# The low parts of float32 weights: subtracted anew for the second sequence, or written to DRAM by the first and loaded by the second

## The chip, the core and the metric

The kernel runs on one core of one Trainium2 chip. The metric is the device time of one execution in microseconds (us). The kernel before has a median of 3235.25 us over 3 runs (3233.89 to 3237.98).

## The reference

Two sequences of 512 tokens and 1024 channels go through a trunk of two layers, with one set of weights for both. A layer is

```python
h = rms_norm(x, ln1_g);  z = h @ w_in            # 1024 -> 2816, split over four mixers
y = [s5(z), hyena(z), rwkv7(z), na(z)]           # 256 channels each
x = x + concat(rms_norm(y_g, grp_g)) @ w_out     # 1024 -> 1024
h = rms_norm(x, ln2_g)
x = x + square(relu(h @ w_mlp1)) @ w_mlp2        # 1024 -> 4096 -> 1024
```

Everything is float32. The mixers are a complex diagonal scan in two directions (S5), a long convolution by spectra (Hyena), a recursion with a state per head in two directions (RWKV-7), and attention in a window of 8 by 16 tokens.

## The kernel before

**Dense products.** Each float32 operand is taken as the sum of two parts: `hi`, the value rounded to 12 significant bits, and `lo`, the rest. `mm3` adds three products for each pair of 128x128 weights and 128x512 activations: w_hi h_hi (L1392), w_hi h_lo (L1393) and w_lo h_hi (L1394). A weight tile is [128, 4, 128], 256 KB, and takes part in 12 matrix multiplications of 512 columns.

**Weights.** `load_w` (L1372 to L1384) loads one tile, raw, and makes both parts: ScalarE (ACT) rounds it to `hi` (`split`, L297), and GpSimd (POOL) or VectorE (DVE) subtracts (L298), so that `lo` lies where the raw tile was. Every fourth tile is subtracted on DVE, the others on POOL. Seven buffers hold tiles: three for `hi`, four for the raw tile that becomes `lo`. A load waits until PE is done with the tile four places before it. For one sequence a layer takes 188 tiles: 44 of w_in, 16 of w_out, 64 of w_mlp1 and 64 of w_mlp2. Each sequence loads and splits all of them in both layers: 376 tiles a sequence, 752 in all.

**Order of the work.** The dense products run as one stream: w_in of the first layer for sequence 0, then for sequence 1; then w_out, the MLP and the next layer's w_in of sequence 0; the same of sequence 1; w_out and MLP of the second layer of sequence 0; of sequence 1. The mixers of one sequence run beside the dense products of the other. A scheduler sets each engine's order when the program is built; on the chip each engine goes through its own queue in order. SyncE (SP) issues every DMA, in order: a DMA whose wait is not over holds up those behind it. In the MLP a tile of results leaves PSUM by DVE (L1535, and L1536 squares it), is split by ACT (L297) and DVE (L298), and w_mlp2's products are added to x by DVE (L1545).

Of the kernel before, what the change touches and what calls it, by code (L numbers as in the profile page):

```python
# [5 lines left out]
F32 = mybir.dt.float32  # L6
# [6 lines left out]
P = 128  # L13
T = 1024          # tokens: both sequences, side by side
# [9 lines left out]
ROUND = 12582912.0          # 1.5 * 2**23: adding and taking it off rounds to an integer  # L24
# [3 lines left out]
# vectors by channel of one layer, packed as columns of a [128, NPAR] tile  # L28
# [19 lines left out]
def tiled(w, nk, n):  # L48
    """[DEPTH, K, N] -> [DEPTH, N / n, K / (128 nk), 128, nk, n]: what one transfer takes lies together."""
    L, k, m = w.shape  # L50
    return w.reshape(L, k // (P * nk), nk, P, m // n, n).transpose(0, 4, 1, 3, 2, 5)


# [1 line left out]

def pack_params(inp):
    """[DEPTH, 128, NPAR_IN]: column j of a vector holds its channels 128 j .. 128 j + 127."""
    out = np.zeros((DEPTH, P, NPAR_IN), np.float32)
    for n, c in _PAR:
        a = np.asarray(inp[n])  # L60
        for l in range(DEPTH):
            v = a[l].reshape(-1)
            if n in ('na_q_g', 'na_k_g'):
                v = np.concatenate([v, v])
            out[l, :, POFF[n]:POFF[n] + c] = v.reshape(c, P).T
    return out


def s5_layout(inp):
    """[DEPTH, 128 (group parity, state), ...]"""  # L70
# [3 lines left out]
    def sc(x):          # (L, 2, 16, 64) -> (L, 128, 16 = (pair, dir))  # L74
        return x.reshape(DEPTH, 2, 8, 2, 64).transpose(0, 3, 4, 2, 1).reshape(DEPTH, P, 16)

    def mb(x):          # (L, 2, 16, 64, 16) -> (L, 128, 16, 16)
        return x.reshape(DEPTH, 2, 8, 2, 64, 16).transpose(0, 3, 4, 2, 1, 5).reshape(DEPTH, P, 16, 16)
# [7 lines left out]
def na_bias(inp):  # L86
    """[DEPTH, head pair, 128 queries (row, col 16), case 3, head 2, 256 keys (row 8, col 32)]: the table's entries
    by position, the constant -1e30 outside the window."""
# [16 lines left out]
def constants():  # L105
# [13 lines left out]
    # DFT at the half-odd multiples of 1/1024 below 1/8, tokens 4 s + j  # L119
    th = 2 * np.pi * (np.arange(128) + 0.5) / 1024  # L120
    ang = np.arange(512)[:, None] * th[None]
    cs = np.stack([np.cos(ang), -np.sin(ang)], 1).reshape(128, 4, 2, 128)       # s, j, (re, im), f
    c['hy_fw'] = np.concatenate([cs, -cs[:, 3:]], 1)
    c['hy_iv'] = (cs * (2.0 / 1024)).transpose(3, 1, 2, 0)                      # f, j, (re, im), s
# [11 lines left out]
def place(nc):  # L136
    """Where the memory that Mem hands out begins: it ends with SBUF."""
# [5 lines left out]
class Mem:  # L143
    """Parts (lo, hi) of the big tile, in units of 1 KB per partition, the first ones preferred: views are
    handed out and given back in program order, and Tile orders the accesses to them."""
# [48 lines left out]
class Ctx:  # L194
    """Pools, constants and small helpers shared by the parts of the kernel."""
# [46 lines left out]
    def rsqrt(self, x, n, tag):  # L242
        """x [128, n] (SBUF) -> 1/sqrt(x): a first guess by the exponent, within 3.5%; a step of third order (the
        best coefficients for that range), which leaves 3e-5; and one of Newton."""
# [15 lines left out]
    def token_rstd(self, srcs, ntok, sel, add, tag, sc=1.0, mulc=None):  # L260
        """srcs: squares, tiles [128 ch, ntok]; sums over the channels that sel [128, w] picks (and over
        the tiles if w is 1) -> 1/sqrt(sums * sc + add), [128 tok, ntok / 128, tiles * w]."""
# [16 lines left out]
    def head_bcast(self, rn, M, tag):  # L279
        """rn [128 tok, 4, heads 2] view of one channel tile -> PSUM [128 ch, 512 tok]."""  # L280
# [9 lines left out]
    def bcast(self, rn, pb):  # L290
        """rn [128 tok, n] -> PSUM pb [128, n * 128], the same on every partition."""
# [3 lines left out]
    def split(self, hi, lo, x, eng):  # L295
        """hi + lo = x: hi has 12 significant bits, lo the rest."""
# [10 lines left out]
# A step works on 8 chunks at once: 4 of the forward direction (slots 0-3) and 4 of the backward one  # L307
# (slots 4-7, in token order); two steps a sequence. The two recursions over chunks run side by side.

def rw_shift(K, par, zp, i, out):  # L310
    """zp [128, 514], zero at the ends -> out = (1 - mu) z + mu / 2 (prev + next)."""
# [7 lines left out]
def rw_load(K, zr, i, n, M):  # L319
    """n tiles of channels of one sequence."""  # L320
# [5 lines left out]
def rw_seq(K, l, par, zr, M):  # L326
    """One sequence. zr: DRAM [1024 ch, 512 tok] (r, k, v, wd + ad, gd, shifted) -> [128, 2, 512]."""
    nc = K.nc
    k = rw_load(K, zr, 2, 2, M)
    # kk / 2, normalised over each head  # L330
# [31 lines left out]
def rw_wa(K, l, zr, M):  # L362
    """What the decays and a are made of, in two parts: [128, 2, (w2 over a2 | tanh wd over ad), 512]."""
# [3 lines left out]
    w2 = ww[:, 0].rearrange("p (d c) -> p d c", d=2)        # rows 0-63: w2, rows 64-127: a2  # L367
# [10 lines left out]
def rw_step(K, l, par, g, zr, prep, y, st, M, beside):  # L378
    """Forward chunks 4 g .. 4 g + 3, backward ones 7 - 4 g .. 4 - 4 g; y [128, 2, 512] is set (g = 0)
    or added to (g = 1); st: the states [128, 2 dir, 2 tiles, 64]. Returns the new ones. beside: a generator,  # L380
    run beside the chunks."""
    nc = K.nc

    def tok(x):             # [128, 512] by token -> [128, dir, 256]
        x = x.rearrange("p (d t) -> p d t", d=2)
        return x[:, ::-1] if g else x

    def tok4(x):            # -> [128, dir, 4 chunks, 64]
# [3 lines left out]
    def s3(x):              # by slot  # L392
# [9 lines left out]
    for c in range(2):  # L402
# [16 lines left out]
        # log decays / -exp(-1/2), summed up within the chunk  # L419
# [6 lines left out]
        ep = ep_[:, :, 0:66]        # columns 0 and 65 are 1  # L426
# [8 lines left out]
        b_t = M([P, 8, 2, 64])      # (b, k) on the even head's partitions, (k, b) on the odd one's  # L435
# [23 lines left out]
    # scores of every slot and head, by token of b or k (partitions) and of a or r  # L459
# [15 lines left out]
    # inverse of I - N, the backward ones transposed: first its blocks of 16, one on each partition (block in the pair,  # L475
    # slot, tile, parity, pair); a 64 x 64 matrix takes 4160 words, so that the blocks of the diagonal lie 1040 apart
    d1 = K.d([32 * 4160], "rw_d1", 2)               # slot, tile, parity
# [38 lines left out]
    # blocks of 32: with R1, R2 on the diagonal and Q of N off it, R1 Q R2 is off it; half of R1's rows a partition  # L516
# [22 lines left out]
    rc = M([P, 2, 16, 32])          # (parity, pair, row); the inverse, its transpose; (slot, tile), column  # L539
# [13 lines left out]
    # blocks of 64: rows lo that N's block has, columns hi that it fills  # L553
# [39 lines left out]
    # values by token: even heads at partitions 64.., odd heads at 0..; U fills the other half  # L593
# [19 lines left out]
    # what the values add to W  # L613
# [13 lines left out]
    # the chunks, one after the other  # L627
    for i in range(4):
        next(beside, None)
        sl = slice(i, 8 - i, 7 - 2 * i)         # slots i and 7 - i  # L630
# [58 lines left out]
def rw_bonus(K, l, par, zr, out, M):  # L689
    """The bonus and the gate, [128, 2, 512] each."""  # L690
# [52 lines left out]

def s5_ops(K, l, M, tag):
    """Operators of one layer, to DRAM: B [128 (t, c), pair, re/im, dir, 128], C [128 (re/im, n), pair,
    parity, dir, 128 (t, c)], lag matrices [16 groups, 16 c, 15 lags x 16]. Returns them and a^8."""
# [23 lines left out]
    # (a - 1) / lambda  # L770
# [15 lines left out]
    def pairs(re, im):  # L786
        """[re | re] and [im | -im]: products with (x, y), the second's halves swapped, add up."""
# [12 lines left out]
    GD = K.d([4, 2, 2, 16, 240], f"s5_gd{l}")        # pair % 4, pair // 4, parity, c, lags  # L800
    for half in range(2):
        yield from s5_half(K, l, half, f2, a2, sB, sC, GD, M, tag)
    # a^8 for the recursion over chunks, laid out (ri, pair, dir)
# [17 lines left out]
def s5_half(K, l, half, f2, a2, sB, sC, GD, M, tag):  # L821
    """The operators of 4 of the 8 pairs of groups."""
# [8 lines left out]
    def cmul(out, x, ri, conj):  # L831
        """out = x * (r + i im), views [128, 8 (ri, pair), 2 (dir), 16]."""
# [16 lines left out]
    for j in range(8):  # L849
        bj = BAv[:, :, 7 - j:9 + j:2 * j + 1]        # forwards at 7 - j, backwards at 8 + j  # L850
# [21 lines left out]
    for j in range(9):  # L872
        cj = CAv[:, :, j:18 - j:17 - 2 * j]          # forwards at j, backwards at 17 - j
# [14 lines left out]
    # lag matrices  # L888
# [25 lines left out]
def s5_front(K, l, zd, M):  # L914
    """One sequence. zd: DRAM [16 groups, 16 c, 8 t, 64 chunks] -> the inputs by chunk and the states."""
# [3 lines left out]
    SS = M([P, 2, 8, 130])          # the forward states at 1 .. 64, the backward ones at 65 .. 128  # L919
# [33 lines left out]
    # from (parity, n), re/im to (re/im, n), parity  # L953
# [10 lines left out]
def s5_back(K, l, par, zd, front, M, tag):  # L964
    """Returns [128, 2, 512]."""
# [3 lines left out]
    ys = M([P, 8, 4, 2, 16])        # (pair // 4, chunk), t, pair % 4, parity, c  # L969
    for q in range(2):  # L970
        L = M([P, 8, P])            # pair % 4, pair // 4
# [3 lines left out]
        py = K.p([P, 4, P], tag)   # (pair // 4, chunk), pair % 4, (t, c)  # L975
        for j in range(4):
            Cop = M([P, 2, 2, P])   # pair // 4, dir
# [28 lines left out]
    # gelu(x) = x (1 + tanh(sqrt(2/pi) (x + 0.044715 x^3))) / 2  # L1006
# [9 lines left out]
    for c in range(2):  # L1016
# [6 lines left out]
        # columns are (t, chunk), the output's (chunk, t)  # L1023
# [8 lines left out]
def reduce_angle(K, x, k):  # L1032
    """x -> x - 2 pi round(x / 2 pi), within [-pi, pi]; k: scratch like x."""
# [795 lines left out]
```

## Time and profile before

The profiled execution has a span of 3230.3 us from its first to its last instruction; the profile gives no other time of its own for it. The three timed runs lie 3.6 to 7.7 us above that span.

| engine | busy us | share of the span |
|---|---|---|
| PE (TensorE) | 2989.3 | 93% |
| DVE | 2222.3 | 69% |
| POOL | 1222.8 | 38% |
| ACT | 1054.7 | 33% |

From the order of SP's loads the dense stream stands so in the trace (start of the first load of each piece, us): w_in of layer 1 for sequence 0 at 6 and for sequence 1 at 226; w_out 472, MLP 658 and w_in of layer 2 at 1217, all for sequence 0; the same for sequence 1 at 1403, 1478 and 2043; then w_out 2239 and MLP 2310 of sequence 0, and w_out 2819 and MLP 2861 of sequence 1, which is the end. So the second sequence's tiles are loaded from 226 to 472, from 1403 to 2239 and from 2819 on.

A busy share is a mean over stretches with different limits, so the stretches are looked at apart. PE's busy time counts waiting inside a matrix multiplication's own latency too; in the last stretch, where PE has nothing but dense products, one of 512 columns starts every 0.227 us. DMA counts are of the core's 16 DMA engines together.

### The profile page before, as it was taken

The numbers are of one execution on the slowest core, as the hardware profiler recorded it, in microseconds if no ns is written. First come the engines' busy times: TensorE is split into PE (matmuls) and PEld (weight loads), VectorE is DVE, ScalarE is ACT, GpSimd is POOL, SyncE is SP. The second block draws the span as 40 slices with busy tenths as digits, with TensorE's granted clock in tenths as the row PEclk, the third lists the DMA queues.
The fourth block names the chain that finished last, engine by engine and source line by source line (L and its number), as shares of the span: only waits on it lengthen the run. The fifth ranks groups of instructions, "written<-read, shape, count | busy, mean of one in ns | idle before, by whom it ended". The sixth has DMA issues, their size and how long they took to land.

```text
span 3230.3 us, 48385 instructions
## 1 busy us (share of the span) xinstructions
PE 2989.3 (93%) x17328; PEld 2329.1 (72%) x17328; DVE 2222.3 (69%) x4431; ACT 1054.7 (33%) x1934; POOL 1222.8 (38%) x963
## 2 busy tenths in 40 slices
PE   7998898789899998998889999788999999999999
PEld 5676776667677776676667777677777777888887
DVE  8987993774884879648957366868775486544443
ACT  5333233342222334333222233333332233332222
POOL 6644430332323346453333233443333243343333
PEclk9999888799999999998999999899989999999999
DMA  5464253252334334543324333346234333433333
GB/s 162 145 160 151 98 144 93 74 115 77 89 100 143 92 117 140 153 144 93 90 72 106 102 115 108 105 137 167 76 74 117 111 115 101 126 110 98 95 98 108
DMA packets 361397, 365.23 MB, mean 113 GB/s; under 512 B 175014, under 2 KB 215590, under 8 KB 360136
## 3 DMA queue, kind: packets, MB, share of 16 engines
q1 hardware_dynamic: 361160, 362.14, 38.6%
q8 instruction: 140, 2.29, 0.3%
q14 instruction: 97, 0.79, 0.1%
HBM read 305.06 MB, written 54.10 MB: 111 GB/s over the span
## 4 chain that ended last, share of the span: by engine, by line
PE 39%; DVE 14%; DMA 2%; issue 2%; ACT 1%; SPq 1%; POOL 0%; DVEq 0%; ACTq 0%; POOLq 0%
PE pd L1392 10%; PE pd L1394 10%; PE pd L1393 10%; DVE m L1167 1%; DVE m L298 1%; PE ra L675 1%; DVE m L530 1%; PE ra L673 1%; PE ra L467 1%; DVE m L950 1%; DVE m L512 1%; DVE s_t L946 1%; DVE s_t L949 1%; DVE m L1545 1%; DVE do L1535 0%
## 5 line engine op out<-in xcount | busy, mean ns | idle before, releaser
L298 POOL TENSOR_TENSOR m<-m,m 128x512 fp32r<-128x512 f32 x564 | 793.4, 1409 | 1480.2 <-ACT m L297 1432.4
L1392 PE MATMUL pd<-m,m 128*128 128x512 f32 x2984 | 1225.8, 411 | 108.1 <-ACT m L297 36.0
L1394 PE MATMUL pd<-m,m 128*128 128x512 f32 x2984 | 1212.6, 407 | 14.9 <-POOL m L298 9.8
L1393 PE MATMUL pd<-m,m 128*128 128x512 f32 x2984 | 1211.9, 406 | 2.7 <-DVE m L298 2.1
L297 ACT CAST m<-m 128x512 fp32r<-128x512 f32 (+1 forms) x776 | 488.2, 632 | 1112.8 <-PE pd L1393 401.7
L1392 PEld LDWEIGHTS pd<-m,m 128*128 128x128 f32 x2984 | 581.8, 195 | 264.7 <-issue 68.9
L1394 PEld LDWEIGHTS pd<-m,m 128*128 128x128 f32 x2984 | 581.3, 195 | 160.9 <-POOL m L298 16.3
L1393 PEld LDWEIGHTS pd<-m,m 128*128 128x128 f32 x2984 | 581.4, 195 | 132.8 <-issue 9.1
L1545 DVE TENSOR_TENSOR m<-pd,m 128x512 f32<-128x512 f32 x256 | 175.1, 686 | 234.7 <-PE pd L1394 234.1
L298 DVE TENSOR_TENSOR m<-m,m 128x512 fp32r<-128x512 f32 (+1 forms) x212 | 172.6, 814 | 116.6 <-ACT m L297 116.1
L1535 DVE SCALAR_TENSOR_TENSOR do<-pd,R 128x512 f32<-128x512 f32 x128 | 87.7, 687 | 112.5 <-PE pd L1394 104.3
L297 ACT CAST m<-do 128x512 fp32r<-128x512 f32 x128 | 79.4, 620 | 237.2 <-DVE do L1536 237.1
L1167 DVE TENSOR_TENSOR m<-m,m 128x512 f32<-128x512 f32 (+1 forms) x224 | 154.2, 724 | 1.1 <-POOL m L1167 0.8
L298 DVE TENSOR_TENSOR m<-do,m 128x512 fp32r<-128x512 f32 x128 | 101.5, 794 | 45.1 <-ACT m L297 44.5
L1536 DVE TENSOR_TENSOR do<-do 128x512 f32<-128x512 f32 x128 | 129.5, 1013 | 2.6
L467 PE MATMUL ra<-m,m 64*128 64x128 f32 x512 | 73.4, 335 | 22.1 <-DVE m L451 12.4
L467 PEld LDWEIGHTS ra<-m,m 64*128 64x128 f32 x512 | 62.7, 229 | 37.8 <-issue 20.4
L946 DVE TENSOR_TENSOR s_t<-m,s_AI 128x32 f32<-128x32 f32 x252 | 81.6, 324 | 7.3 <-ACT m L935 1.8
L950 DVE TENSOR_TENSOR m<-m,s_t 128x32 f32<-128x32 f32 x252 | 83.1, 330 | 5.0
L675 PE MATMUL ra<-m,m 128*64 128x64 f32 x512 | 79.0, 248 | 0.0
L840 POOL TENSOR_TENSOR m<-m,s5p_i 128x256 f32<-128x256 f32 x64 | 57.8, 903 | 55.0 <-DVE m L842 31.1
L1423 DVE SCALAR_TENSOR_TENSOR m<-m,par,m 128x512 fp32r<-128x512 f32 x64 | 67.4, 1062 | 15.9 <-ACT m L1422 15.8
(351 smaller groups left out, 3609.5 us busy)
## 6 DMA issues: line engine op xcount, KB each, us to landing
m<-in_w_mlp SPq DMA_DIRECT2D x512, 256.0 KB, 2.6
m<-in_w_in SPq DMA_DIRECT2D x176, 256.0 KB, 2.8
m<-zr SPq DMA_DIRECT2D x36, 512.0 KB, 4.0
m<-in_w_out SPq DMA_DIRECT2D x64, 256.0 KB, 2.9
m<-in_xT SPq DMA_DIRECT2D x32, 256.0 KB, 4.3
zr<-do SPq DMA_DIRECT2D x32, 256.0 KB, 2.1
m<-hy_spec SPq DMA_DIRECT2D x8, 1024.0 KB, 5.1
m<-s_sB SPq DMA_DIRECT2D x16, 512.0 KB, 4.2
```

The lines of the kernel that those rows point to most:

```text
L297: self.nc.scalar.copy(out=hi, in_=x)
L298: eng.tensor_tensor(out=lo, in0=x, in1=hi.bitcast(F32), op=SUB)
L467: nc.tensor.matmul(out=pm[q][:, ch - c2, c], lhsT=bk[c][h, ch].rearrange("p a b -> p (a b)"), rhs=ar[c][h, ch].rearrange("p a b -> p (a b) ...
L675: nc.tensor.matmul(out=py[b0:b0 + 64, d, c], lhsT=uv[:, ch, c, q], rhs=sr[:, ch, 2 * c + q], start=st is None, stop=True)
L946: nc.vector.tensor_tensor(out=t2.rearrange("p q (x d) -> p (q x) d", d=2), in0=pv, in1=AIv, op=MUL)
L950: nc.vector.tensor_tensor(out=cv, in0=cv, in1=t1, op=ADD)
L1167: eng.tensor_tensor(out=o, in0=a, in1=b, op=op)
L1392: K.nc.tensor.matmul(out=ps, lhsT=wh, rhs=hh, start=(i == 0), stop=False)
L1393: K.nc.tensor.matmul(out=ps, lhsT=wh, rhs=hl, start=False, stop=False)
L1394: K.nc.tensor.matmul(out=ps, lhsT=wl, rhs=hh, start=False, stop=(i == n - 1))
L1536: nc.vector.tensor_tensor(out=r, in0=r, in1=r, op=MUL)
L1545: nc.vector.tensor_tensor(out=x[m], in0=ps, in1=x[m], op=ADD)
```

## The change

`load_w` is given a key (name of the array and indices) in place of a slice. The first time that it sees a key, it loads and splits as before, and then writes `lo` to a DRAM tile of its own. The second time, which is the second sequence, it loads the raw tile and the low part with two DMAs, and ACT rounds the raw tile in place; there is no subtraction. For these tiles all seven buffers form one ring, of which each tile takes two in turn (raw and `hi` share one, `lo` has the other). The diff also takes out comments and docstrings, and the callers pass keys.

```diff
-def load_w(K, src):
+def load_w(K, key):
     nc = K.nc
     sh = [P, 4, P]
-    hi = K.W.view(NMEM + 2 * (K.nw % NHI), sh, F32R)
-    o = NMEM + 2 * (NHI + K.nw % (NW - NHI))
-    raw, lo = K.W.view(o, sh, F32), K.W.view(o, sh, F32R)
+    src = K.A[key[0]][key[1:]]
+    n = K.nw
+    K.nw += 1
+    again = key in K.lows
+    i, j = (2 * n % NW, (2 * n + 1) % NW) if again else (n % NHI, NHI + n % (NW - NHI))
+    hi, lo = (K.W.view(NMEM + 2 * o, sh, F32R) for o in (i, j))
+    raw = K.W.view(NMEM + 2 * (i if again else j), sh, F32)
     K.tc.cur_priority -= OFF_W
-    nc.sync.dma_start(out=raw, in_=src)
-    K.nw += 1
-    K.split(hi, lo, raw, nc.vector if K.nw % LO_V == 0 else nc.gpsimd)
+    if again:
+        nc.sync.dma_start(out=raw, in_=src)
+        nc.sync.dma_start(out=lo.bitcast(F32), in_=K.lows[key])
+        nc.scalar.copy(out=hi, in_=raw)
+    else:
+        nc.sync.dma_start(out=raw, in_=src)
+        K.split(hi, lo, raw, nc.vector if K.nw % LO_V == 0 else nc.gpsimd)
+        K.n += 1
+        d = K.lows[key] = K.d(sh, f"lo_{K.n}")
+        nc.sync.dma_start(out=d, in_=lo.bitcast(F32))
     K.tc.cur_priority += OFF_W
     return hi, lo
```

The built program has 968 instructions on POOL before and 686 now, 4433 and 4339 on DVE, 1526 and 2278 DMAs on SP; ACT and PE have as many as before.

First place: SP, in the MLP of layer 2 for sequence 0 (first use of the tiles), before. Names are buffers; a raw tile is loaded from in_w_mlp.

```order
L1380 DMA m2876_24329<-in_w_mlp2 128x512
L1274 DMA m2630_22679<-zn1_1664_18725 128x512
L1380 DMA m2879_24349<-in_w_mlp2 128x512
L1380 DMA m2882_24369<-in_w_mlp2 128x512
L1380 DMA m2885_24389<-in_w_mlp2 128x512
L1160 DMA m2644_22785<-zh1_1663_18724 128x2x512
```

The same place now; a tile's `lo` is the buffer numbered one below its raw buffer (both are the same memory), and lo_... is DRAM.

```order
L1390 DMA m2883_25022<-in_w_mlp2 128x512
L1394 DMA lo_2808_2809_25004<-m2879_24999 128x512
L1390 DMA m2886_25044<-in_w_mlp2 128x512
L1394 DMA lo_2811_2812_25026<-m2882_25021 128x512
L1390 DMA m2889_25066<-in_w_mlp2 128x512
L1394 DMA lo_2814_2815_25048<-m2885_25043 128x512
L1390 DMA m2892_25088<-in_w_mlp2 128x512
```

Between two loads now stands the write of the tile before the first of them: a tile's load follows in the queue on the write of the tile two places before it.

Second place: SP, in the MLP of layer 1 for sequence 1 (second use), before.

```order
L1380 DMA m1944_16872<-in_w_mlp1 128x512
L1380 DMA m1947_16878<-in_w_mlp1 128x512
L322 DMA m1586_13601<-rw_kk_1142_12426 128x2x512
L322 DMA m1587_13603<-zr0_1105_11971 128x2x512
L1380 DMA m1951_16915<-in_w_mlp2 128x512
```

The same two loads of the mixer (L322) now.

```order
L1387 DMA m1926_17213<-lo_1200_1201_10197 128x512
L1386 DMA m1931_17251<-in_w_mlp1 128x512
L322 DMA m1586_14065<-rw_kk_1554_12838 128x2x512
L322 DMA m1587_14067<-zr0_1481_12347 128x2x512
L1387 DMA m1930_17250<-lo_1204_1205_10236 128x512
L1386 DMA m1934_17257<-in_w_mlp1 128x512
L1387 DMA m1933_17256<-lo_1206_1207_10244 128x512
L1386 DMA m1938_17294<-in_w_mlp1 128x512
```

Raw and low loads alternate; a mixer's loads stand between those of one tile.

Third place: POOL, in the same MLP (layer 1, sequence 1), before. L439, L444, L451 and L665 are steps of RWKV-7, L298 is the subtraction.

```order
L439 TENSOR_TENSOR m_13637<-m_13603,m_13630 128x8x64
L444 TENSOR_TENSOR m_13642<-m_13642,m_13325 128x512
L451 TENSOR_TENSOR m_13638<-m_13642,m_13633 64x8x64
L298 TENSOR_TENSOR m_16916<-m_16915,m_16914 128x512
L427 MEMSET m_13674 128x8x2
L298 TENSOR_TENSOR m_16936<-m_16935,m_16934 128x512
L444 TENSOR_TENSOR m_13686<-m_13686,m_13325 128x512
L439 TENSOR_TENSOR m_13681<-m_13603,m_13674 128x8x64
L665 TENSOR_TENSOR rw_se_14960<-rw_st_13538,rw_ec_13605 128x256
```

The same steps now.

```order
L439 TENSOR_TENSOR m_14101<-m_14067,m_14094 128x8x64
L444 TENSOR_TENSOR m_14106<-m_14106,m_13781 128x512
L451 TENSOR_TENSOR m_14102<-m_14106,m_14097 64x8x64
L427 MEMSET m_14138 128x8x2
L444 TENSOR_TENSOR m_14150<-m_14150,m_13781 128x512
L439 TENSOR_TENSOR m_14145<-m_14067,m_14138 128x8x64
L665 TENSOR_TENSOR rw_se_15424<-rw_st_13998,rw_ec_14069 128x256
```

POOL has the mixers' steps alone there.

## Rows read from the trace of the kernel before

**Rows 1.** Windows: busy us by engine, TensorE clock, DMA share, GB/s

```profile
0.00:230.00 230.00, 197.59 (x891) 142.04 (x892) 203.89 (x430) 91.69 (x153) 131.45 (x114) 0.93 0.53 155
230.00:480.00 250.00, 225.95 (x1611) 176.92 (x1608) 223.23 (x540) 83.64 (x167) 99.82 (x81) 0.89 0.45 131
480.00:665.00 185.00, 154.28 (x1102) 117.40 (x1101) 110.50 (x258) 63.89 (x128) 43.08 (x36) 0.80 0.31 88
665.00:1410.00 745.00, 690.18 (x4122) 533.51 (x4121) 532.72 (x1048) 242.63 (x448) 285.46 (x230) 0.95 0.39 113
1410.00:2245.00 835.00, 759.22 (x4536) 589.63 (x4535) 583.32 (x1153) 267.06 (x494) 305.98 (x236) 0.94 0.39 111
2245.00:2825.00 580.00, 563.23 (x3319) 440.13 (x3318) 394.23 (x780) 186.64 (x354) 202.67 (x156) 0.96 0.36 107
2825.00:3230.00 405.00, 398.85 (x1763) 329.49 (x1761) 174.36 (x229) 119.11 (x194) 154.30 (x113) 1.00 0.34 102
```

**Rows 2.** The chain that ended last, shares of the span by engine

```profile
PE 39%; DVE 14%; DMA 2%; issue 2%; ACT 1%; SPq 1%; POOL 0%; DVEq 0%; ACTq 0%; POOLq 0%
```

**Rows 3.** That chain's earliest piece: start us, us, what

```profile
1319.57 1.03 DVE do L1477
```

**Rows 4.** PE's waits, 1410:2245: us in total, times, longest

```profile
PE pd L1392 <- DVE do L1535: 16.5, 5, 8.0
PE ra L467 <- DVE m L451: 11.6, 3, 8.3
PE pd L1392 <- DVE m L1545: 9.9, 5, 2.9
```

**Rows 5.** Groups by line, 230:480: count, busy us, mean ns, idle before

```profile
L298 POOL TENSOR_TENSOR m<-m,m 128x512 fp32r<-128x512 f32 x35 | 48.8, 1399 | 74.3 <-ACT m L297 72.8 <-issue 1.1
L298 DVE TENSOR_TENSOR m<-m,m 128x512 fp32r<-128x512 f32 x11 | 8.3, 757 | 0.2 <-ACT m L297 0.2
```

**Rows 6.** Groups by line, 1410:2245

```profile
L298 POOL TENSOR_TENSOR m<-m,m 128x512 fp32r<-128x512 f32 x141 | 204.4, 1453 | 409.2 <-ACT m L297 393.8 <-issue 13.2 <-DVE do L1535 1.6
L298 DVE TENSOR_TENSOR m<-m,m 128x512 fp32r<-128x512 f32 x46 | 36.3, 788 | 36.1 <-ACT m L297 36.1
```

**Rows 7.** Single lines: ns min/median/max of one instruction, first and last start

```profile
L1536 DVE TENSOR_TENSOR do<-do x128: 657/692/1830, 692.4 to 3204.3; 128x512 f32<-128x512 f32 x128
L950 DVE TENSOR_TENSOR m<-m,s_t x252: 183/216/1347, 298.6 to 2321.2; 128x32 f32<-128x32 f32 x126
L946 DVE TENSOR_TENSOR s_t<-m,s_AI x252: 184/208/1325, 298.1 to 2320.1; 128x32 f32<-128x32 f32 x126
L1545 DVE TENSOR_TENSOR m<-pd,m x256: 669/691/694, 729.1 to 3226.0; 128x512 f32<-128x512 f32 x128
```

**Rows 8.** Groups by line, whole span

```profile
L1536 DVE TENSOR_TENSOR do<-do 128x512 f32<-128x512 f32 x128 | 129.5, 1013 | 2.6
L950 DVE TENSOR_TENSOR m<-m,s_t 128x32 f32<-128x32 f32 x252 | 83.1, 330 | 5.0
L946 DVE TENSOR_TENSOR s_t<-m,s_AI 128x32 f32<-128x32 f32 x252 | 81.6, 324 | 7.3 <-ACT m L935 1.8
```

**Rows 9.** The page's list of DMAs: KB each, us to landing; its queue's load

```profile
m<-in_w_mlp SPq DMA_DIRECT2D x512, 256.0 KB, 2.6
q1 hardware_dynamic: 361160, 362.14, 38.6%
```

**Rows 10.** Waits of SP's queue and of ACT, whole span

```profile
SPq L1380 <- PE pd L1394: 1558.1, 566, 12.7
ACT m L297 <- PE pd L1393: 401.7, 178, 9.5
```

**Rows 11.** Single lines: the load's issue, the rounding, the subtraction

```profile
L1380 SPq DMA_DIRECT2D m<-in_w_mlp x512: 322/328/1708, 658.1 to 3215.2; - x171
L297 ACT CAST m<-m x776: 601/621/1059, 11.6 to 3218.0; 128x512 fp32r<-128x512 f32 x190, 128x1024 fp32r<-128x1024 f32 x4
L298 POOL TENSOR_TENSOR m<-m,m x564: 1252/1292/4282, 13.0 to 3216.9; 128x512 fp32r<-128x512 f32 x188
```

More of the change, by code (lines that the diff above doesn't have):

```diff
@@ L1395, in mm3, with dense @@
     K.tc.cur_priority -= OFF_P
-def dense(K, src, h, tag="pd"):
-    w = [load_w(K, src[kh]) for kh in range(2)]
+def dense(K, key, h, tag="pd"):
+    w = [load_w(K, key + (kh,)) for kh in range(2)]
     ps = K.p([P, S], tag)
@@ L1480, in w_in @@
         for i in range(n):
-            fn(i, dense(K, K.A['w_in'][l, off + i], hp, tags.pop() if tags else "pd"))
+            fn(i, dense(K, ('w_in', l, off + i), hp, tags.pop() if tags else "pd"))
             yield
@@ L1513, in w_out @@
             nc.sync.dma_start(out=x, in_=xsrc[m * P:m * P + P])
-        w = [load_w(K, K.A['w_out'][l, m, kh]) for kh in khs]
+        w = [load_w(K, ('w_out', l, m, kh)) for kh in khs]
         ps = K.p([P, S], "pd")
@@ L1531, in first @@
     def first(f):
-        ps = dense(K, K.A['w_mlp1'][l, f], hp)
+        ps = dense(K, ('w_mlp1', l, f), hp)
         t = M([P, 2, S], F32R)
@@ L1541, in second @@
         for m in range(8):
-            wh, wl = load_w(K, K.A['w_mlp2'][l, m, e])
+            wh, wl = load_w(K, ('w_mlp2', l, m, e))
             ps = K.p([P, S], "pd")
@@ L1603, in trunk @@
         K = Ctx(tc, base, sb, ps, dr, A)
-        K.s5w, K.hys, K.nw, K.nz = {}, {}, 0, 0
+        K.s5w, K.hys, K.lows, K.nw, K.nz = {}, {}, {}, 0, 0
         K.W = K.mem()
```

## The prediction

> **What bounds the kernel now.** The table of stretches comes first, because the busy share of the whole span hides what differs [rows 1]. The reader is to see three kinds. From 2825 us on PE is busy for 398.85 of 405 us at the full clock with DVE at 43% (174.36): dense products alone set the pace there, and nothing that makes weights cheaper can shorten it. From 2245 to 2825 PE is idle for 17 us of 580. In the other stretches PE is idle for 32, 24, 31, 55 and 76 us, its granted clock is 0.80 to 0.95 of the full one, and DVE is busy for 89% (0 to 230 and 230 to 480), 60%, 72% and 70% of the time. Second, who ends PE's waits from 1410 to 2245: DVE in the three longest groups, two of them the evacuations of PSUM that stand in DVE's queue behind the mixers' work [rows 4]. Third, the chain of work that ended last [rows 2]. Its shares add up to about 59%, since it is followed back only to 1319.57 us [rows 3]. DVE's 14% of 3230 us is thus 452 us within the 1911 us that the chain covers; almost none of it can lie after 2825, so DVE holds 452 of 1505 us, 30%, between 1320 and 2825. In the stretches with mixers the bound is PE and DVE by turns.
>
> **What the change removes.** The second sequence's 376 subtractions go. Those that matter are in the two stretches where it runs beside mixers; the rest lies after 2825, where PE is full anyway.
>
> - DVE's own: 11 of 8.3 us [rows 5] and 46 of 36.3 us [rows 6].
> - POOL's: 35 of 48.8 us [rows 5] and 141 of 204.4 us [rows 6]. POOL is no bound (306 of 835 us busy from 1410 to 2245 [rows 1]), so this counts only for what it does to DVE.
>
> It does something. The squaring of a hidden tile (L1536, SBUF to SBUF) takes 657 ns at least and 692 in the median, but 1830 at most and 1013 in the mean; the scan's products of 32 columns take 183 and 184 ns at least, 1347 and 1325 at most, 330 and 324 in the mean [rows 7, 8]. The excess at most, 1.1 to 1.2 us, is close to one POOL subtraction, 1252 to 1292 ns [rows 11]. L1545, of the same size as L1536 but with an operand from PSUM, never leaves 669 to 694 ns [rows 7]. So a DVE instruction with two operands in SBUF waits for a POOL instruction that is under way. The Trainium skill says this outright (SBUF — State Buffer, section "SBUF: two separate sides": the port pair that the two engines share is held for a whole instruction); by it alone up to the whole of the removed 253 us of POOL's time could come back to DVE; the rows bound it better.
>
> How much of POOL's time DVE loses is not a row, so it is bounded. The three lines lose 128 x (1013 - 657) + 252 x (330 - 183) + 252 x (324 - 184) ns = 45.6 + 37.0 + 35.3 = 118 us over POOL's 1222.8 us (the POOL column of rows 1, added up): 0.10 us for each us of POOL at least. At most it is 1. The three are 294 us of DVE's 2222 and lose 40% of it; were half of DVE's work of that kind, it would be 0.36 of POOL's time. I take 0.3, an estimate nearer to the measured end: 0.3 x 48.8 = 15 us and 0.3 x 204.4 = 61 us (by the lower bound 5 and 20).
>
> DVE is thus relieved of 8 + 15 = 23 us from 230 to 480, and of 36 + 61 = 97 us from 1410 to 2245. What is on the path: the chain has DVE for 30% of the time, 251 of 835 us, while DVE is busy for 583, so 0.43 of its work, 42 us of the 97. Late next is PE itself, which has only 76 us of idle time to give there, and the loops over the mixers' steps whose PE and ACT parts stay. I take two thirds: **28 us**. From 230 to 480 no chain is shown; with the same 0.43 it is **10 us** (PE idle there: 24). Bounds: nothing, if other waits take every place, and 24 + 76 = 100 us, if all PE idle time of the two goes.
>
> The place of the mixers changes too. ACT waits 401.7 us for PE before it rounds, since a `hi` buffer is free only when PE is done with the tile three before [rows 10]; for the second sequence it rounds in place as soon as the raw tile is there, and ACT's queue no longer stands still for that. That is within the bounds above.
>
> **What it adds.** 376 writes and 376 loads, 256 KB each, 197 MB on top of 362 [rows 9]. An issue takes 0.33 us of SP [rows 11]; 188 loads and their pairs in 835 us make 124 us of it, and SP spends half the span waiting for PE anyway (1558.1 us [rows 10]), so issue alone is hidden. The engines' share goes from 38.6% to about 38.6 x 559 / 362 = 60%. In the last stretch a matrix multiplication takes 405 / 1763 = 0.23 us [rows 1], so a tile of 12 takes 2.76 us; it then moves 512 KB, 190 GB/s, against the 102 at a share of 0.34 there: some 0.63. The low part is loaded when PE has finished with the tile three before, about 6.0 us before PE wants it (two tiles and the next one's first two products), and landing takes 2.6 us [rows 9]. So no stall is expected after 2825. Elsewhere the mixers' own DMAs, 2% of the chain or 65 us [rows 2], land later behind more traffic: I take a tenth, **6 us**; bounds 0 and, if landing grows with the bytes (54%), 35.
>
> The writes add a wait on SP: a tile's write waits for its subtraction, and the load two tiles on, and mixers' DMAs, stand behind it. Its cover: load, rounding and subtraction take 2.6 + 0.62 + 1.29 = 4.5 us [rows 9, 11], while two tiles take 2 x 510 / 128 = 8.0 us in the MLP from 2315 to 2825, 2 x 560 / 128 = 8.8 in that from 665 to 1225 and 2 x 220 / 44 = 10 in w_in at the start. Waits of 3.5 us on ACT and POOL together fit in. I cost it at nothing; bounds 0 and the 62 us that 376 writes of one issue (0.33 us) make when half of it reaches PE.
>
> **Sum.** -28 - 10 + 6 = -32 us. On the profiled execution that is 3230 - 32 = 3198 us of span; the median of the runs lies 5 us above that span, so 3235 - 32 = **3203 us**.
>
> **Rivals.**
>
> 1. *All relief comes through.* DVE is late by POOL at 0.36 or more and PE's idle time closes; the clock, 0.89 and 0.94 in the two stretches, rises with it. For: PE's longest waits there end at DVE [rows 4]. Against: the mixers' steps also wait for PE and DMA. With 60 to 80 of the 100 us: about 3165.
> 2. *Bytes eat the gain.* The mixers' 65 us of DMA on the chain grow by 54%, 35 us, against the 38: 3235 - 38 + 35 = 3232, no change. Against: DMA is busy for 39% from 1410 to 2245 [rows 1]. The Trainium skill's SBUF — State Buffer, "A bandwidth-pool intuition that's wrong", says that HBM is almost always the end-to-end bottleneck; by that rule alone this change would lose. The last stretch, PE full at 102 GB/s, shows that it is not so here before the change.
> 3. *The write becomes a gate (slower).* Place: SP, in the first sequence's MLPs and w_in. If the subtraction is late behind the mixers' work on POOL, or behind DVE at 89%, by more than 3.5 us, the next loads and the mixers' DMAs leave late, in a chain of tile to tile. Suppose a quarter of the 256 MLP tiles and all of w_in's 88 hold SP for one more POOL instruction: (64 + 88) x 1.3 us = 198 us of queue. A quarter of it reaching PE is 49 us, inside the bound of 62. Less the gain of 38 and with the 6: 3235 + 49 - 38 + 6 = 3252. It decides from the point where the extra wait is over 3.5 us a tile. For: SP already waits for half the span, and its order is fixed when the program is built. Against: the cover above.
>
> That the change does not do what it says is excluded by the built program: 282 instructions fewer on POOL, 94 on DVE.
>
> **How the numbers follow.** About 0.2% (6.5 us) is what a measurement here can tell from no change. The forecast, 3180 to 3228, has 0.46; the first rival 0.20; the second 0.10; the third, with whatever the new order on the engines costs, 0.24. Faster is 0.46 + 0.20 = 0.66, the same 0.10, slower 0.24. The range from 3155 to 3258 takes in most of the first rival and the price of the third, and leaves out 0.2. The likeliest case's own range is 3180 to 3228.
>
> **What would show it.** Right: the mean of L1536 and of the scan's products falls towards 0.69 and 0.2 us in the second sequence's stretches and not in the first's; the stretch from w_out of sequence 1 to the end of w_in for it shrinks by some 28 us, w_in of layer 1 for sequence 1 by 10, the last by nothing. Wrong: SP waits long for L298 and ACT then waits longer for raw tiles in the first sequence's stretches; PE waits for the low part's DMA; or the mean of L1536 stays at 1.0 us.

## The result, and the profile after

The changed kernel has a median of 3206.22 us against 3235.25 of the kernel before, 5 runs each: a ratio of 0.9897, 95% interval 0.9872 to 0.9921. The forecast was 3203. One of the five executions, the profiled one, had a mean granted clock of 0.82 and took 3350 us; the ratio leaves it out, and the rows here are from a repeat of the same kernel (median 3196.85, ratio 0.9885, interval 0.9865 to 0.9905; profiled span 3197.9).

The first line of the repeat's page: busy us, share of the span, instructions.

```profile
PE 2974.9 (93%) x17328; PEld 2321.5 (73%) x17328; DVE 2030.3 (63%) x4337; ACT 1053.2 (33%) x1934; POOL 823.4 (26%) x681
```

PE and ACT do what they did; DVE has 192 us less and POOL 399. The 94 instructions that DVE lost took some 0.8 us each [rows 5, 6], 75 us, so over half of its fall is in work that it still does.

To see where the time went, both executions are cut at the same events: the last tile of results of a product leaves PSUM. The pieces are: to the end of w_out of layer 1 for sequence 0; to the end of w_in of layer 2 for it; w_out, MLP and w_in for sequence 1; w_out and MLP of layer 2 for sequence 0; for sequence 1. The windows of the kernel before (columns as in [rows 1]):

```profile
0.00:674.00 674.00, 585.34 (x3626) 441.99 (x3626) 546.55 (x1236) 242.73 (x453) 281.96 (x234) 0.88 0.44 127
674.00:1414.00 740.00, 686.67 (x4108) 531.02 (x4108) 524.44 (x1038) 240.09 (x443) 279.19 (x227) 0.95 0.40 115
1414.00:2259.00 845.00, 767.94 (x4621) 595.67 (x4620) 595.57 (x1199) 271.30 (x507) 307.47 (x237) 0.94 0.39 113
2259.00:2831.00 572.00, 556.51 (x3243) 435.93 (x3242) 384.34 (x737) 184.27 (x344) 202.43 (x156) 0.97 0.36 104
2831.00:3230.00 399.00, 392.85 (x1737) 324.51 (x1735) 171.35 (x225) 116.27 (x190) 151.71 (x111) 1.00 0.34 101
```

The same pieces of the changed kernel:

```profile
0.00:644.00 644.00, 565.12 (x3620) 426.03 (x3621) 500.00 (x1200) 241.32 (x450) 231.38 (x199) 0.91 0.58 175
644.00:1401.00 757.00, 694.71 (x4117) 537.30 (x4116) 528.90 (x1065) 242.78 (x447) 277.68 (x226) 0.94 0.55 172
1401.00:2205.00 804.00, 761.98 (x4695) 593.96 (x4693) 494.27 (x1165) 271.02 (x512) 104.46 (x97) 0.95 0.59 180
2205.00:2795.00 590.00, 557.44 (x3171) 437.77 (x3164) 380.46 (x722) 181.97 (x338) 203.45 (x154) 0.96 0.52 166
2795.00:3198.00 403.00, 395.66 (x1740) 326.43 (x1740) 126.65 (x188) 116.06 (x189) 6.46 (x5) 0.99 0.59 191
```

The pieces change by -30, +17, -41, +18 and +4 us. The third, where the second sequence runs beside mixers, gains 41: PE does the same work (768 and 762 us) and is idle for 42 us in place of 77, with DVE down by 101. Added up over all of PE's waits in that piece, those that end at DVE fall from 67 to 27 us, and those that end elsewhere go from 10 to 15. Both pieces of the first sequence's layers lose 35 together. The sum, -32, is what was forecast; its parts are not.

The borders cut the dense stream and not the mixers beside it. The first piece has 36 DVE instructions fewer, of which 11 are subtractions; the other 25, 14 us of RWKV-7's steps, now stand in the second piece. The third has 74 of PE's instructions more, the fourth 72 fewer. So some of each change is order. The first piece also hides that the stretch which was forecast to lose 10 us, w_in of layer 1 for sequence 1, did not get shorter. Its results leave PSUM in these windows, before and after:

```profile
238.00:487.00 249.00, 225.17 (x1544) 176.87 (x1546) 221.78 (x551) 79.84 (x159) 95.79 (x82) 0.88 0.45 132
259.00:537.00 278.00, 256.48 (x1891) 197.37 (x1889) 207.06 (x596) 90.02 (x186) 54.90 (x51) 0.93 0.54 167
```

It takes 29 us more with 347 more of PE's instructions in it, and w_out, which follows, takes 107 us in place of 187.

Who is late in DVE shows in the squaring of a hidden tile (L1536, L1548 after), here by groups, in the two MLPs from layer 1 of sequence 1 to layer 2 of sequence 0, before:

```profile
L1536 DVE TENSOR_TENSOR do<-do 128x512 f32<-128x512 f32 x32 | 28.9, 905 | 0.3
L1536 DVE TENSOR_TENSOR do<-do 128x512 f32<-128x512 f32 x32 | 33.7, 1053 | 0.7
```

and after:

```profile
L1548 DVE TENSOR_TENSOR do<-do 128x512 f32<-128x512 f32 x32 | 22.1, 689 | 0.7
L1548 DVE TENSOR_TENSOR do<-do 128x512 f32<-128x512 f32 x32 | 32.3, 1008 | 0.7
```

In the sequence that no longer subtracts, the mean falls to 689 ns, about the median of all 128 before (692 ns [rows 7]); in the other it stays near where it was. The scan's two products beside the first of these MLPs fall from 336 and 250 ns to 215 and 207; beside the MLP of sequence 0 in layer 1 they do not fall (300 and 303, now 296 and 340). These are the rows on which the mechanism rests: the instructions are the same, POOL's subtractions are gone. PE's longest waits in the third piece are now shorter than those of before [rows 4]; two of the three end at the mixers' own steps:

```profile
PE ra L561 <- DVE m L548: 10.1, 3, 4.5
PE ra L467 <- DVE m L451: 6.2, 2, 4.0
PE pd L1404 <- issue: 5.9, 6, 2.5
```

DMA, to be read against [rows 9]: a load of w_mlp lands in 2.9 us instead of 2.6, at a share of 56% instead of 39%.

```profile
m<-in_w_mlp SPq DMA_DIRECT2D x512, 256.0 KB, 2.9
lo<-m SPq DMA_DIRECT2D x376, 256.0 KB, 2.2
m<-lo SPq DMA_DIRECT2D x376, 256.0 KB, 2.7
q1 hardware_dynamic: 469448, 559.32, 56.3%
```

SP's queue, to be read against [rows 10]: of 1558 us of waiting for PE 936 are left (with a third group of 48 us, not shown), and 411 us are now waits for the subtraction.

```profile
SPq L1387 <- PE pd L1405: 576.1, 266, 18.4
SPq L1394 <- POOL m L298: 335.2, 211, 5.9
SPq L1390 <- PE pd L1406: 311.6, 186, 7.4
SPq L1394 <- DVE m L298: 75.7, 50, 5.1
```

### The profile page after: what moved, and what is told of

Same layout as the page of the kernel before. It is cut to its first block, busy times and chain, and to the rows that moved or that the text cites. A ratio compares the mean times of both kernels' runs of the same rounds, so it can differ in the third digit from the quotient of the medians.

```text
span 3348.4 us, 49172 instructions
## 1 busy us (share of the span) xinstructions
PE 3189.8 (95%) x17328; PEld 2375.3 (71%) x17328; DVE 2038.6 (61%) x4337; ACT 1058.5 (32%) x1934; POOL 814.2 (24%) x681
## 4 chain that ended last, share of the span: by engine, by line
PE 73%; DVE 16%; DMA 6%; issue 2%; ACT 1%; SPq 1%; POOL 0%; DVEq 0%; ACTq 0%; POOLq 0%
PE pd L1404 18%; PE pd L1405 18%; PE pd L1406 18%; PE ra L675 2%; PE ra L673 2%; DVE m L530 2%; PE ra L467 2%; DVE m L1167 1%; PE ma L1316 1%; DMA m<-in_w_mlp 1%; DVE m L298 1%; DMA m<-in_w_in 1%; DMA m<-rw_D 1%; DVE m L532 1%; PE ra L1198 1%
## 5 line engine op out<-in xcount | busy, mean ns | idle before, releaser
L1404 PE MATMUL pd<-m,m 128*128 128x512 f32 x2984 | 1287.9, 432 | 68.0 <-DVE do L1547 19.9
L1406 PE MATMUL pd<-m,m 128*128 128x512 f32 x2984 | 1278.0, 429 | 5.7 <-DMA m<-lo 2.2
L1405 PE MATMUL pd<-m,m 128*128 128x512 f32 x2984 | 1280.9, 429 | 0.0
L1404 PEld LDWEIGHTS pd<-m,m 128*128 128x128 f32 x2984 | 589.4, 198 | 263.1 <-issue 34.5
L1406 PEld LDWEIGHTS pd<-m,m 128*128 128x128 f32 x2984 | 588.6, 197 | 191.2 <-issue 14.0
L1405 PEld LDWEIGHTS pd<-m,m 128*128 128x128 f32 x2984 | 588.7, 197 | 178.1 <-issue 14.8
L298 POOL TENSOR_TENSOR m<-m,m 128x512 fp32r<-128x512 f32 x282 | 390.2, 1386 | 831.1 <-ACT m L297 767.1
L1388 ACT CAST m<-m 128x512 fp32r<-128x512 f32 x376 | 232.8, 620 | 727.9 <-DMA m<-in_w_mlp 472.2
L297 ACT CAST m<-m 128x512 fp32r<-128x512 f32 (+1 forms) x400 | 256.3, 644 | 594.9 <-PE pd L1405 328.4
L298 DVE TENSOR_TENSOR m<-m,m 128x512 fp32r<-128x512 f32 (+1 forms) x118 | 108.3, 918 | 63.6 <-ACT m L297 58.1
L1167 DVE TENSOR_TENSOR m<-m,m 128x512 f32<-128x512 f32 (+1 forms) x224 | 141.6, 671 | 8.3 <-PE ma L1346 3.8
L298 DVE TENSOR_TENSOR m<-do,m 128x512 fp32r<-128x512 f32 x128 | 94.3, 739 | 53.7 <-ACT m L297 53.2
L1548 DVE TENSOR_TENSOR do<-do 128x512 f32<-128x512 f32 x128 | 106.6, 834 | 2.9
L1428 POOL TENSOR_TENSOR m<-m 128x512 f32<-128x512 f32 x40 | 56.9, 1424 | 120.2 <-ACT m L1427 119.3
L1167 POOL TENSOR_TENSOR m<-m,m 128x512 f32<-128x512 f32 x32 | 48.6, 1521 | 151.6 <-DVE m L1167 113.5
```

Of the source, the lines that this page charges most:

```text
L297: self.nc.scalar.copy(out=hi, in_=x)
L298: eng.tensor_tensor(out=lo, in0=x, in1=hi.bitcast(F32), op=SUB)
L1167: eng.tensor_tensor(out=o, in0=a, in1=b, op=op)
L1388: nc.scalar.copy(out=hi, in_=raw)
L1404: K.nc.tensor.matmul(out=ps, lhsT=wh, rhs=hh, start=(i == 0), stop=False)
L1405: K.nc.tensor.matmul(out=ps, lhsT=wh, rhs=hl, start=False, stop=False)
```

## The experiments

Twelve kernels were run beside the kernel before, in four groups on four chips. The kernel before has medians of 3231, 3239, 3229 and 3237 us in them, so the ratio to the kernel before is what is compared, with its 95% interval.

| kernel | ratio to before | interval | us of 3231 |
|---|---|---|---|
| the changed kernel again | 0.9885 | 0.9865-0.9905 | -37 |
| GpSimd's 282 instructions put back | 1.0040 | 1.0024-1.0056 | +13 |
| VectorE's 94 put back | 0.9907 | 0.9879-0.9935 | -30 |
| one write instead of 376 | 0.9818 | 0.9794-0.9842 | -59 |
| writes of 32 KB | 0.9758 | 0.9728-0.9789 | -78 |
| kernel before with the writes | 1.0037 | 1.0018-1.0055 | +12 |
| the same, writes from ScalarE's queue | 1.0026 | 1.0009-1.0044 | +8 |
| changed, writes from ScalarE's queue | 0.9802 | 0.9773-0.9831 | -64 |
| changed, layer 2's w_out and MLP split twice | 0.9832 | 0.9800-0.9865 | -54 |
| both of these | 0.9804 | 0.9778-0.9830 | -63 |
| both parts written and loaded | 0.9836 | 0.9809-0.9862 | -53 |
| low part loaded before the raw tile | 0.9896 | 0.9862-0.9930 | -34 |

**The changed kernel again.** No edit.

> The changed kernel as it is, for a profile at the usual clock. Theory of the prediction (VectorE is relieved: of its own subtractions and of waiting for GpSimd's): 3190 to 3215 us; in the second sequence's stretches the squaring of a hidden tile takes 0.69 to 0.75 us in the mean, in the first sequence's still 0.9 to 1.1; the stretch from w_out of layer 1 to w_in of layer 2 for the second sequence is about 28 us shorter, w_in of layer 1 for the second sequence about 10 shorter, the last stretch as long as before. Rival (the write is a gate, and what is gained comes from elsewhere): the first sequence's stretches are longer by 10 us or more each, SyncE waits for the subtraction.

The time and the squaring are as the theory has them, the second and the last stretch are not: w_in of layer 1 for the second sequence is 29 us longer, not 10 shorter, and the last piece 4 longer. The rival is half right: the first sequence's pieces are longer, by 17 and 18 us, and SP does wait for the subtraction.

**GpSimd's instructions put back.**

```diff
         nc.scalar.copy(out=hi, in_=raw)
+        if K.nw % LO_V:
+            nc.gpsimd.tensor_tensor(out=lo, in0=lo.bitcast(F32), in1=K.ones.unsqueeze(1).to_broadcast(sh), op=MUL)
```

> The changed kernel, and for three of four tiles of the second sequence GpSimd multiplies the loaded low part by a tile of ones in place: 282 instructions of the size of the subtractions that the change took away from it. Theory of the prediction: 24 of the 38 us gained come from GpSimd's absence, so 3225 to 3240, and the squaring takes 0.85 to 1.05 us in the mean in the second sequence's MLP again. Rival (the gain is VectorE's own 94 subtractions, or the new order; GpSimd was never in the way): 3200 to 3212.

Measured 3243.86 in a group where the changed kernel had 3196.85: the whole gain is gone, 47 us, more than the 24 expected. The third piece takes 835 us (845 before, 804 without these instructions); its window:

```profile
1411.00:2246.00 835.00, 766.53 (x4704) 592.59 (x4704) 561.31 (x1178) 271.64 (x513) 310.20 (x236) 0.95 0.56 173
```

and two groups in it, the added instruction and the squaring:

```profile
L1390 POOL TENSOR_TENSOR m<-m,c_ones 128x512 fp32r<-128x512 f32 x139 | 201.8, 1453 | 417.5 <-DMA m<-lo 215.7 <-PE pd L1407 40.9 <-PE pd L1408 33.7
L1550 DVE TENSOR_TENSOR do<-do 128x512 f32<-128x512 f32 x32 | 26.4, 829 | 0.4
```

Nothing was added to DVE, yet it is busy for 561 us against 494: 67 us for 202 of POOL's, 0.33 us for each. Taken one by one, the 1164 DVE instructions of that piece take 66 us longer. Over the whole span it is 0.25 (99 us for 403). The squaring is back at 829 ns. The multiplication also stands before PE's use of the low part, as the subtraction did, and PE waits for it, and longer for the low part's load than in the changed kernel (the last of these lines):

```profile
PE pd L1408 <- POOL m L1390: 8.1, 9, 1.8
PE pd L1408 <- DMA m<-lo: 9.6, 3, 5.8
PE pd L1406 <- DMA m<-lo: 2.6, 2, 1.8
```

PE's idle time in this piece grows by 26 us against the changed kernel: 10 in waits that end at DVE (37 us, 27 in the changed kernel, 67 before), 16 in waits that end at POOL or at a DMA. So this edit has a price of its own on PE. It shows DVE's loss in full, but not that all 47 us come by way of DVE.

**VectorE's instructions put back.** The same edit with `nc.vector` and `if K.nw % LO_V == 0`.

> The changed kernel, and for one of four tiles of the second sequence VectorE multiplies the loaded low part by a tile of ones in place: 94 instructions of the size of VectorE's own subtractions that the change took away. GpSimd's 282 stay away. Theory, mended after the same was done for GpSimd (which gave back 47 us): VectorE's own 45 us of work in the two stretches count by the same 0.43, about 20 us, so 3208 to 3222. Rival (only GpSimd was in the way, VectorE has room): 3195 to 3204.

Measured 3207.19, ratio 0.9907 against 0.9885: 7 us, and the intervals overlap. The expected 20 is not reached; of the two terms VectorE's own is the small one. The third piece is no longer with them than without (795 and 804 us), and PE's waits there that end at DVE stay at 26 us.

**The writes left out.** Later loads take the first tile's low part.

```diff
-        K.n += 1
-        d = K.lows[key] = K.d(sh, f"lo_{K.n}")
-        nc.sync.dma_start(out=d, in_=lo.bitcast(F32))
+        if not K.lows:
+            K.n += 1
+            K.one = K.d(sh, f"lo_{K.n}")
+            nc.sync.dma_start(out=K.one, in_=lo.bitcast(F32))
+        K.lows[key] = K.one
```

> The changed kernel with one write of a low part instead of 376; every later load of a low part takes that one tile (the low products of the second sequence are therefore those of one tile's low part, left so to keep the loads). Theory of the prediction: the writes cost next to nothing, so 3200 to 3210, at most 6 us under the changed kernel. Rival, the write as a gate on SyncE's queue: the changed kernel loses 50 us to it, so this runs at 3155 to 3170.

Measured 3176.39, 20 us under the changed kernel in the same group: over three times the 6 that was forecast, under half of the gate's price.

**The writes alone**, on the kernel before (its buffers and its splitting for both sequences). The diff is against the changed kernel; the write after the first split stays.

```diff
-    i, j = (2 * n % NW, (2 * n + 1) % NW) if again else (n % NHI, NHI + n % (NW - NHI))
+    i, j = n % NHI, NHI + n % (NW - NHI)
     ...
     if again:
         nc.sync.dma_start(out=raw, in_=src)
-        nc.sync.dma_start(out=lo.bitcast(F32), in_=K.lows[key])
-        nc.scalar.copy(out=hi, in_=raw)
+        K.split(hi, lo, raw, nc.vector if K.nw % LO_V == 0 else nc.gpsimd)
```

> The kernel before with the 376 writes alone: the second sequence still splits its own tiles and loads no low parts. Theory of the prediction: the price of the writes alone, 0 to 6 us, so 3235 to 3242. Rival, the gate: 3270 to 3290. A third view (the order that the scheduler makes is worth more than any of the parts): anything from 3215 to 3255.

Measured 3243.74 against 3230.83: 13 us, between the theory and the gate, and inside the third view's wide range. Its first piece ends at 661 us, 13 earlier than before, though nothing is taken off any engine there: the scheduler's order differs, and 32 DVE instructions of that piece (15 us) stand in the next one. So some 13 of the changed kernel's 30 us in that piece can come with the order, not with the relief. The third piece, in which nothing is written, stays as it was (843 us, 845 before), so a new order alone did not shorten it here.

**Small writes**: the wait stays, the bytes go. As with one write, later loads all take the first tile's low part; every other tile of the first sequence has this write:

```diff
+            d = K.d([P, 64], f"lo_{K.n}")
+            nc.sync.dma_start(out=d, in_=lo[:, 0, 0:64].bitcast(F32))
```

> As the kernel with one write in place of 376, and each later tile of the first sequence writes 64 of its 512 columns, 32 KB instead of 256, to a DRAM tile that nobody reads (the low products of the second sequence are one tile's, left so). The wait of SyncE for the subtraction is there 376 times, the bytes are gone (12 MB in place of 99). If the writes' 20 us are the wait on SyncE's queue (the gate): 3192 to 3202, like the changed kernel. If they are the bytes: 3174 to 3182, like the kernel with one write.

Measured 3159.44, ratio 0.9758: in neither range, and below even the kernel with one write (0.9818), which has less to write and no such wait. No price of writes can explain that; the order of work differs too. SP waits for the subtraction as long as in the changed kernel (411 us there):

```profile
SPq L1398 <- POOL m L298: 323.1, 214, 5.3
SPq L1398 <- DVE m L298: 87.2, 56, 6.2
```

So the wait on SP is there in full and the loss is not: the gate as it was costed, 49 us, falls.

**Writes from ScalarE's queue.** `nc.scalar.dma_start` in place of `nc.sync.dma_start` for the write.

> The changed kernel with the 376 writes issued by ScalarE's queue instead of SyncE's: the wait for the subtraction stands before ScalarE's next work, not before the next loads. If the wait on SyncE's queue is the price and ScalarE, busy a third of the time, can bear it: 3178 to 3190. If it is the bytes: 3195 to 3200. If the wait only changes its place, since ScalarE rounds the next tiles and serves the mixers: 3200 to 3230.

Measured 3174.45, ratio 0.9802: the same bytes, and 27 us less than from SP. It looked as if the place in SP's queue were the price. The writes alone from that queue were to tell:

> The kernel before with the 376 writes alone, issued by ScalarE's queue; the second sequence still splits its own tiles. On SyncE's queue the same writes cost 13 us (ratio 1.0037 to the kernel before). If the price of a full-size write is its place in SyncE's queue: 0.998 to 1.001 of the kernel before. If it is the bytes themselves, or the price only showed in that kernel's order of work: 1.003 or more.

Measured 3240.91 against 3228.97, ratio 1.0026, beside 1.0037 from SP: no difference that these intervals show. The place in the queue is no general price either. In the traces, some 20 of the 23 us that the changed kernel gains by the other queue are in one piece, the fourth (569 us in place of 590).

**Layer 2's w_out and MLP split by both sequences.**

```diff
-        K.n += 1
-        ...
+        if key[0] == 'w_in' or key[1] < DEPTH - 1:
+            K.n += 1
+            ...
```

> The changed kernel, but the second layer's w_out and MLP are split by both sequences, as before the change: their 144 low parts are neither written nor loaded, and the second sequence subtracts them in the last stretch, where no mixer runs. If the writes cost what the first runs show (12 us in each of the two MLPs of the first sequence) and the last stretch has room for the subtractions: 10 to 14 us under the changed kernel, 3182 to 3188. If what the writes cost is elsewhere, or the last stretch needs the relief: 3195 to 3205.

Measured 3186.69, ratio 0.9832. In the traces the fourth piece is 581 us (590 in the changed kernel) and the last 398 (403): where PE is full, the second sequence loses nothing by subtracting again, and loses a little, 5 us, by loading instead.

```profile
2205.00:2786.00 581.00, 554.52 (x3165) 436.45 (x3166) 383.27 (x721) 180.92 (x337) 205.14 (x156) 0.96 0.35 103
2786.00:3184.00 398.00, 392.73 (x1736) 324.45 (x1735) 172.16 (x225) 116.69 (x190) 150.86 (x111) 1.00 0.34 101
```

Together with the other queue:

> The changed kernel with the writes on ScalarE's queue and without those of the second layer's w_out and MLP, which both sequences split themselves. If the two savings are of different things (10 us of writes in the second layer's MLP, 3 us of loads in the last stretch, and 20 us or more of place in the queue elsewhere): 0.974 to 0.979 of the kernel before. If the writes on ScalarE's queue are free already, only the last stretch's 3 us are left: 0.979 to 0.981.

Measured 3171.18, ratio 0.9804: no better than the other queue alone (0.9802). Both are faster than the kernel before and than the changed kernel. The fourth piece takes 568 us here and 581 in the kernel just above, and neither writes nor loads a low part in it: its products are the same, the order of the mixers' steps beside them is not.

**Both parts written and loaded**, no rounding the second time. The lines cut off at the end write `hi` beside `lo`.

```diff
-        nc.sync.dma_start(out=raw, in_=src)
-        nc.sync.dma_start(out=lo.bitcast(F32), in_=K.lows[key])
-        nc.scalar.copy(out=hi, in_=raw)
+        nc.sync.dma_start(out=hi.bitcast(F32), in_=K.lows[key][0])
+        nc.sync.dma_start(out=lo.bitcast(F32), in_=K.lows[key][1])
         ...
```

> The changed kernel, but the first sequence writes both parts (752 writes of 256 KB) and the second loads both and rounds nothing: 376 roundings of 0.62 us leave ScalarE. ScalarE is busy for a third of the time, so its relief should be worth little, 0 to 5 us, and 376 more writes on SyncE's queue cost another 13 to 20: 0.992 to 0.997 of the kernel before. If ScalarE's rounding stands on the path: below 0.985.

Measured 3182.08, ratio 0.9836: with twice the writes it is faster than the changed kernel. Its fourth piece is as long as the changed kernel's, 590 us, at a DMA share of 0.69 instead of 0.52; its third is 786 against 804:

```profile
1392.00:2178.00 786.00, 751.52 (x4682) 587.36 (x4680) 487.81 (x1160) 164.00 (x326) 98.81 (x92) 0.95 0.60 183
2178.00:2768.00 590.00, 555.64 (x3160) 436.45 (x3160) 376.23 (x720) 177.57 (x333) 197.41 (x154) 0.96 0.69 227
```

So bytes written do not add up to time. Whether the gain is that of ACT's roundings is not shown: PE's waits that end at ACT are only 6 us in the third piece of the changed kernel, and the order differs here too.

**The two loads in the other order.**

> The changed kernel with the second sequence's two loads in the other order: first the low part, then the raw tile. Same instructions, same bytes, same writes; what changes is when the raw tile can be issued (it now waits behind the low part's buffer, about one tile later) and the order that the scheduler makes of it. If the sizes seen so far (13 to 20 us for the writes) are of the edits themselves: 0.986 to 0.991 of the kernel before, like the changed kernel. If orders of work alone scatter kernels of one content by 10 to 20 us: outside that, on either side.

Measured 3200.97, ratio 0.9896, the changed kernel's: this change of order moves nothing.

## Why the prediction was right, and where it was not

**The mechanism and the size of DVE's relief were right.** DVE was to be relieved of 97 us from 1410 to 2245, 36 its own and 61 by POOL's absence. The piece shows 101, of which 67 come back with POOL's instructions alone, which leaves 34. The factor that was guessed at 0.3 us of DVE for each us of POOL measures 0.33. That this relief of DVE is POOL's and not a matter of the new order is shown by the kernel in which POOL's instructions alone are put back. That PE gains by it shows in PE's waits that end at DVE in the third piece: 67 us before and 61 with the writes alone, 27 in the changed kernel and 26 with VectorE's instructions back, 37 with POOL's. How many of the 41 us are POOL's part stays open, since POOL's added step holds up PE by itself as well.

**The share on the path was too small for that stretch.** The chain gave 0.43 and 42 us, and the prediction took two thirds of it, 28. Measured is 41 of 101, 0.41. PE did have the idle time to give: 77 us fell to 42. The discount of a third was the mis-sized step: 28 us forecast, 41 measured.

**The first stretch was right by half at most.** Forecast 10 us in w_in of layer 1 for sequence 1, which got 29 longer; the piece around it got 30 shorter. With the writes alone that piece also gets shorter by 13, with POOL's instructions put back by 20. So 10 to 17 us may be the relief, and the rest is how the scheduler laid out the first 670 us, which the prediction did not count at all. PE is idle for 10 us less in that piece; the other 20 are a shorter busy time at a granted clock of 0.91 in place of 0.88.

**What it adds was mis-sized: 6 us forecast.** The pieces of the first sequence lose 35 us, and the last 4. Leaving the writes out gives back 20 us, and on the kernel before they cost 12. So the step that costed the writes at nothing was wrong, by 12 to 20 us; the 41 us of the small writes are more than leaving the writes out gives, and so no measure of their price. Its worry was wrong as well: the wait on SP grew to 411 us and costs nothing that the small writes show. That the last stretch bears the loads was nearly right, 4 to 5 us for 0. The 6 us were for the mixers' DMAs: PE's waits that end at a DMA are 4.5 us before and 16.3 after, 7.3 more for the mixers' loads and 4.5 for low parts, none of these in the last piece.

The 35 us are not all a price of the writes. Into the second piece came the 14 us of RWKV-7's steps. In the fourth PE is as busy as before (557 us) and idle for 33 us in place of 15, and 8.3 us of that is one wait for a step of RWKV-7, which it does not have there in the kernel before:

```profile
PE ra L467 <- DVE m L451: 8.3, 1, 8.3
```

The kernel that splits layer 2's w_out and MLP twice has the same line in that piece and takes 581 us there, though it writes and loads no low part in it. So some 9 of the 18 us came with the order.

**Rivals.** The first (all relief comes through) is not borne out: in the third stretch 35 of PE's 77 us of idle time went and the granted clock went from 0.94 to 0.95. The 71 us of the first and third piece lie in its 60 to 80, but 13 to 20 of them are not relief. The second (bytes eat the gain) is not shown: twice the written bytes left the fourth piece at 590 us. The third's mechanism, the gate, is not what costs time, though a loss near its size is there. The mechanism of the gain was right; that the sum came out as forecast was luck: by pieces, a gain too small by 33 us (71 in the first and third piece, 38 forecast) and a loss too small by 33 (39 for 6) met, and some of both is work that crossed a border.

**What stays open** is what the writes cost by. It is not the wait, not in proportion to the bytes, and not the queue alone, which was worth 27 us in one kernel and 4 in another, less than its interval tells from nothing. Each of these edits also gives another order of the engines' work. The one edit of order that was tried moved nothing, but the fourth piece, with the same products and no low parts, took 568 and 581 us, and small writes ran 0.6% faster than one write: order is worth as much here as the price that is sought.

## What to carry to other kernels

An engine that is idle for 60% of the time can still be the cause that a busy one is late: look at the spread of one repeated instruction (minimum, median, maximum) and at whether the maximum exceeds the minimum by one instruction of the other engine. Work that is moved to DMA pays where such an engine sets the pace and not where PE is full, so store and reload only there. And a total that comes out right says nothing of its terms: cut both executions at the same events before believing the sum.

## What was not expected of the hardware

Moving 376 writes of 256 KB from SyncE's queue to ScalarE's made one kernel faster by 0.8%; in another the 0.1% is within the intervals. ACT issued them beside its own work at no visible price (ratio 0.9802). And taking 376 roundings of 0.62 us from ACT, an engine busy for a third of the time, went with a gain of 0.5% (0.9836 against 0.9885) although it doubled the writes.
